# Differences of x made beside its sums, and a seventh weight unit for a raw tile and a sum tile

## The chip, the cores and the metric

The kernel runs on one core of one Trainium2 chip. The metric is the device time of one execution in microseconds. The kernel before took 1086.38 us (median of three runs, 1085.44 to 1087.5). A core has five engines with instruction streams of their own: TensorE (PE, with its weight loads PEld), VectorE (DVE), ScalarE (ACT), GpSimd (POOL) and SyncE (SP, which here only issues DMAs). Each works through its stream in the order in which the program was compiled, and they wait for each other by semaphores.

## The reference

One step of a two-layer encoder on 512 + 64 = 576 tokens of width 1024. Layer 0 mixes tokens by causal pooling, layer 1 by attention over selected keys; each is followed by an MLP. Cut to what matters here:

```python
def _mlp(h, w_up, w_down):          # h: (B, T, 1024), w_up: (1024, 4096), w_down: (4096, 1024)
    u = jax.nn.relu(h @ w_up)
    return (u * u) @ w_down
...
for i in range(DEPTH):              # DEPTH = 2
    h = _rmsnorm(x, norm_mix[i])
    ...                             # pooling mixer or attention
    x = x + y.astype(x.dtype)
    x = x + _mlp(_rmsnorm(x, norm_mlp[i]), mlp_w_up[i], mlp_w_down[i]).astype(x.dtype)
```

## The kernel before, in words

**Tiles.** Activations lie transposed: 128 of the 1024 features in the partitions, 576 tokens along the free axis, in two halves of HT = 288. `x[k]` is the residual's k-th block of 128 features (k from 0 to 7). Each fp32 operand of a matmul is split into a high part and the rest, both in the type float32r, and a product is three matmuls: high by high, high by low, low by high.

**Weights.** A weight block of 128 x 1024 is loaded as two raw tiles of 128 x 512 (`Stream.fill`, L199; the load is L213 on the SP queue for the MLPs). `split_unit` (L179) makes of each 128 x 512 piece a *unit*: ACT casts it to `wh` (L181), DVE subtracts to get `wl` (L182). A unit takes a pair of buffers out of a ring of UNITS = 6 pairs (`unit`, L169). Raw tiles come from two pools, RAWS = (4, 3): four `raws` for everything, three of `more` while an MLP or the pooling mixer runs. `fill` issues a load as soon as a raw tile is given back (`done`, L222).

**Sevens.** Most of an MLP is computed by a scheme with seven products in place of eight for a 2 x 2 block product (`seven`, L523). Its weight operands are made from a pair of blocks ("even" and "odd"), seven units for each pair in this order: a11, s1, s2, a12, s3, s2, a22 (`made`, L241). s3 comes about in the raw tile itself: POOL issues a DMA that adds the even block's first half onto the loaded raw tile (L217). s1 is loaded into a *sum tile* by SP (L237), and POOL's DMA adds the other half (L238). s2 is a sum tile too, made by DVE: s1 + a11 (L260), and, once it has been used for the first time, with a12 added (L264). The pool `sums` has four tiles.

The seven products of a seven go into three PSUM banks: a, b and c. The order is b11 into b (then ACT copies b to a, L533), t1 into c, t2 into b, b21 into a, t3 into b, b22 into c, t4 into b. After products a callback reads the bank. In the first matrix (`Up`, L586) `c` and `b` copy banks into `snap` (L599, L602, ACT); `lo0`, `hi1` (L612), `hi0` (L618) and `lo1` run relu and scale on DVE (L595), squares on ACT (L454), sums of the results on DVE (L484 to L491), and the splits of the results, upper on ACT (L473) and lower on DVE (L476). In the second matrix (`Down`, L555) every callback adds to or subtracts from the residual (L562, DVE). `take()` takes the next unit, `ahead()` (L509) makes one more unless `LEAD` units are ready.

**Chunks.** An MLP runs over four chunks of 1024 hidden features. Chunk 0's Up is eight plain blocks (`project`, L297, L677 to L691), followed by four Down sevens in the order FIRST_DOWN. Chunks 1, 2 and 3 are four Up sevens and four Down sevens each (in the last layer chunk 3 has three, and the rest goes with the final norm).

**Operands of x.** The sevens of Up need, for each of four pairs j (blocks j and j + 4 of x), three sums and one difference of scaled quarters of x. `x_sums` (L424) makes the three sums: ACT scales one quarter (L429, into `first`), DVE makes three scalar_tensor_tensors out of x (L430 to L432), and the result is split (L433, L434). This runs for j = 0 and 1 after plain blocks 3 and 5 (L689), in a tile `rough`, and for j = 2 and 3 after the first and second Down seven (`x_prepared`, L694). `x_difference` (L436) takes the split quarters out of `xs`: a subtraction of both parts at once (L439, 576 columns), the sum of the two results (L440), and the split (L441, L442) over the quarter in `xs` that is no longer needed. All four j run after the third Down seven. `snap` is the buffer of the norm's sum of squares (tag "s2"), allocated after the plain blocks (L692).

**Order.** Only some parts of the kernel have an order written by hand. In the MLPs the framework puts each engine's instructions in order by its own simulated timeline, with the program's order as priority, so that an instruction whose operands are ready can be put ahead of earlier ones. A tile is allocated when an earlier tile of its pool has been given back.

**Memory.** Pools lie on top of each other like a stack. `more` lies at the bottom during layer 0's MLP; in attention `under` takes its place, with the cosine table `cs`, the sine table `sn`, a mask and one score tile (6144 bytes per partition, like three raw tiles).

## Time and profile before

| | us |
|---|---|
| median of three runs | 1086.38 |
| lowest, highest | 1085.44, 1087.5 |
| the profiled execution | 1085.9 |
| its span, first to last instruction | 1084.1 |
| PE busy in the span | 1051.9 |
| DVE busy | 909.1 |
| ACT busy | 627.1 |
| POOL busy | 264.6 |

The page names the engine, the line and the tiles of instructions: `wl<-raw,wh` is an instruction that writes `wl` from `raw` and `wh`. "Busy" is the time in which an engine executes; an arrow in square brackets gives idle time of the engine just before an instruction, and what ended it. PE's matmuls overlap, so that a record of 0.30 us follows the one before it after 0.13 us.

In time the span divides so: pooling mixer until about 41 us; layer 0's plain Up blocks until 95, its chunks until 414; attention until about 690; layer 1's MLP with the final norm until the end. The DMA queues moved 157.66 MB, a mean of 145 GB/s.

### The profile page before, as it was taken

The numbers are of one execution on the slowest core, as the hardware profiler recorded it, in microseconds if no ns is written. First come the engines' busy times: TensorE is split into PE (matmuls) and PEld (weight loads), VectorE is DVE, ScalarE is ACT, GpSimd is POOL, SyncE is SP. The second block draws the span as 40 slices with busy tenths as digits, with TensorE's granted clock in tenths as the row PEclk, the third lists the DMA queues.
The fourth block names the chain that finished last, engine by engine and source line by source line (L and its number), as shares of the span: only waits on it lengthen the run. The fifth ranks groups of instructions, "written<-read, shape, count | busy, mean of one in ns | idle before, by whom it ended". The sixth has DMA issues, their size and how long they took to land.

```text
span 1084.1 us, 21647 instructions
## 1 busy us (share of the span) xinstructions
PE 1051.9 (97%) x7942; PEld 1024.0 (94%) x7942; DVE 909.1 (84%) x1845; ACT 627.1 (58%) x1240; POOL 264.6 (24%) x285
## 2 busy tenths in 40 slices
PE   9999999999999999999999999999999999999996
PEld 8999998999999999999988888999999999999895
DVE  7788989879978987869999944688989879979974
ACT  8555466447546654444477776455467447547641
POOL 4100111111111100237686892000111111111001
PEclk9999999999999999999989999999999999999998
DMA  8343676676676654447632454333676666667512
GB/s 252 94 102 89 171 166 151 166 163 169 151 166 165 156 161 165 128 153 191 201 108 68 129 170 123 126 108 97 166 165 157 162 164 165 154 170 161 125 51 88
DMA packets 94459, 157.66 MB, mean 145 GB/s; under 512 B 13729, under 2 KB 25296, under 8 KB 94352
## 3 DMA queue, kind: packets, MB, share of 16 engines
q1 hardware_dynamic: 68720, 109.80, 33.3%
q0 software_dynamic: 15840, 28.84, 17.1%
q10 hardware_dynamic: 9792, 17.63, 5.2%
q8 instruction: 62, 1.02, 0.4%
q14 instruction: 45, 0.37, 0.1%
HBM read 141.15 MB, written 10.89 MB: 140 GB/s over the span
## 4 chain that ended last, share of the span: by engine, by line
PE 78%; DVE 9%; ACT 3%; POOL 3%; issue 3%; DMA 2%; SPq 0%; DVEq 0%; POOLq 0%; ACTq 0%
PE b L504 28%; PE c L504 15%; PE up L305 9%; PE a L504 7%; PE pj L305 7%; PE wo L305 2%; DVE wl L182 2%; PE wa L305 1%; PE pb L1011 1%; PE sc L1284 1%; PE dn L305 1%; PE pt L1310 1%; POOL p L1263 1%; DVE u L476 1%; PE o L1342 1%
## 5 line engine op out<-in xcount | busy, mean ns | idle before, releaser
L181 ACT CAST wh<-raw 128x512 fp32r<-128x512 f32 (+1 forms) x316 | 194.8, 620 | 232.6 <-PE b L504 75.4
L182 DVE TENSOR_TENSOR wl<-raw,wh 128x512 fp32r<-128x512 f32 (+1 forms) x294 | 205.9, 703 | 38.6 <-ACT wh L181 30.2
L504 PE MATMUL b<-u,wh 128*128 128x288 f32 x992 | 203.1, 296 | 2.2 <-ACT a L533 1.7
L504 PEld LDWEIGHTS b<-u,wh 128*128 128x128 f32 x992 | 159.5, 188 | 4.3 <-ACT a L533 3.6
L181 ACT CAST wh<-sum 128x512 fp32r<-128x512 f32 x165 | 101.4, 620 | 80.3 <-PE b L504 36.3
L504 PE MATMUL b<-u,wl 128*128 128x288 f32 x496 | 145.5, 296 | 0.0
L182 DVE TENSOR_TENSOR wl<-sum,wh 128x512 fp32r<-128x512 f32 x165 | 112.0, 687 | 20.6 <-ACT wh L181 18.5
L238 POOL DMA_DIRECT2D sum<-in_w_down x31 | 27.1, 891 | 327.4 <-DVE u L476 86.6
L504 PE MATMUL c<-u,wh 128*128 128x288 f32 x496 | 103.3, 297 | 0.9 <-DVE u L476 0.6
L504 PEld LDWEIGHTS b<-u,wl 128*128 128x128 f32 x496 | 92.8, 188 | 0.0
L305 PE MATMUL up<-xs,wh 128*128 128x288 f32 x512 | 89.6, 296 | 1.0 <-DVE x L1477 0.8
L504 PE MATMUL b<-xt,wh 128*128 128x288 f32 x384 | 77.9, 296 | 8.0 <-DVE v L612 8.0
L476 DVE TENSOR_TENSOR u<-v,u 128x864 fp32r<-128x864 f32 (+2 forms) x100 | 82.1, 825 | 0.9 <-ACT u L473 0.5
L504 PEld LDWEIGHTS c<-u,wh 128*128 128x128 f32 x496 | 80.1, 188 | 2.5 <-DVE x L562 1.5
L473 ACT CAST u<-v 128x864 fp32r<-128x864 f32 (+2 forms) x100 | 72.7, 730 | 8.8 <-DVE v L491 5.4
L504 PE MATMUL b<-xs,wh 128*128 128x288 f32 x384 | 76.8, 295 | 0.0
L305 PEld LDWEIGHTS up<-xs,wh 128*128 128x128 f32 x512 | 74.6, 188 | 2.0 <-ACT wh L181 1.0
L504 PE MATMUL c<-u,wl 128*128 128x288 f32 x248 | 73.2, 295 | 0.0
L238 POOL DMA_DIRECT2D sum<-in_w_up x24 | 20.7, 863 | 209.4 <-DVE wl L182 132.5
L504 PEld LDWEIGHTS b<-xt,wh 128*128 128x128 f32 x384 | 61.3, 188 | 9.6 <-DVE v L612 9.6
L454 ACT ACTIVATE v<-v 128x288 f32<-128x288 f32 (+1 forms) x112 | 52.0, 476 | 16.5 <-DVE v L595 14.1
L305 PE MATMUL pj<-xs,wh 128*128 128x288 f32 x352 | 61.3, 295 | 0.0
(287 smaller groups left out, 2738.4 us busy)
## 6 DMA issues: line engine op xcount, KB each, us to landing
raw<-in_w_up SPq DMA_DIRECT2D x128, 256.0 KB, 3.0
raw<-in_w_down SPq DMA_DIRECT2D x128, 256.0 KB, 2.9
raw<-in_w_o ACTq DMA_DIRECT2D x32, 256.0 KB, 2.8
sum<-in_w_down SPq DMA_DIRECT2D x31, 256.0 KB, 2.9
sum<-in_w_down POOLq DMA_DIRECT2D x31, 256.0 KB, 4.5
raw<-in_w_down POOLq DMA_DIRECT2D x31, 256.0 KB, 5.0
raw<-in_w_in ACTq DMA_DIRECT2D x30, 256.0 KB, 3.0
sum<-in_w_up SPq DMA_DIRECT2D x24, 256.0 KB, 3.0
```

The costliest lines, as they stand in the source:

```text
L181: act.copy(h, src)
L182: how["sub"].tensor_tensor(l, src, f32(h), ALU.subtract)
L238: pool.dma_start(s1, odd[:, 512:], accum_op=ALU.add)
L305: pe.matmul(pt[h][:, :m] if isinstance(pt, tuple) else pt[:, h, :m], wt, xs[k][:, part, c:c + m], start=(k == 0 and i == 0), stop=(k == n ...
L454: act.activation(v, v, AF.Square)
L473: act.copy(u[:, f, 0], v[:, f])
L476: dve.tensor_tensor(u[:, f, 1], v[:, f], f32(u[:, f, 0]), ALU.subtract)
L504: pe.matmul(bank[:, :HT], wt, ut, start=first and j == 0 and i == 0, stop=j == 3 and i == 2, skip_group_check=True)
L1011: pe.matmul(pt[:, c0:c0 + rhs.shape[1]], lhs, rhs, start=n == 0, stop=n == len(steps) - 1)
L1263: pool.tensor_scalar(p, p, rs[:, h:h + 1], 1.0, ALU.mult, ALU.mult)
L1284: pe.matmul(pt[:, hh, :nw], q[:, 2 * s + hh], ks[g][:, part, :nw], start=part == 0, stop=part == 1)
L1310: pe.transpose(pp[:, c:c + P], pr[:, hh, kt * P:(kt + 1) * P], ident)
```

## The change

Four things change together.

1. `x_sums` gets one more output, the difference: a scalar_tensor_tensor out of x and `first` (gain of block j + 4 times its first quarter, minus `first`). `x_difference` only splits what was made there. For j = 0 and 1 the difference waits in `snap`, which is therefore allocated after plain block 3; for j = 2 and 3 it lies in the fifth row of the scratch tile. `x_difference` now runs for j = 0 and 2 after the first Down seven and for j = 1 and 3 after the second, and no longer after the third.
2. A pool `extra` with one pair of weight buffers exists during the MLPs, and every seventh MLP unit is put there, so that the ring has seven pairs. LEAD goes from 5 to 6.
3. The pool `more` has two raw tiles and not three, `sums` three and not four. One raw tile and one sum tile have the size of the pair of weight buffers.
4. `under` must have the size of two raw tiles: the sine table moves into the pool `cst2`, and a pad of 64 columns that nobody uses fills up.

```diff
--- before.py
+++ after.py
@@ -44,10 +44,11 @@
 UNITS = 6
 SPREAD_AT = 5
 SPARE_UNITS = 6
-RAWS = (4, 3)
+UNDER = 64
+RAWS = (4, 2)
 MLP_BLOCKS = ("up", "even", "odd", "down")
 SEEDED = 4
-LEAD = 5
+LEAD = 6
 UP_ORDER = (0, 4, 1, 5, 2, 6, 3, 7)
 FACTORS = ("t4", "t3", "t1", "t2", "b11", "b22", "b21")
 FIRST_DOWN = (0, 2, 1, 3)
@@ -134,7 +135,7 @@
         def __getitem__(self, k):
             return self.t[k // 2][:, k % 2]
 
-    turns = {"spare": 0}
+    turns = {"spare": 0, "extra": 0}
 
     def raw_tile(pool=raws, n=2 * 264):
         return pool.tile([P, n], F32, tag="raw", name=uid("raw"))
@@ -166,8 +167,12 @@
     ready = []
     how = {"sub": dve}
 
-    def unit(n=512):
-
+    def unit(n=512, mlp=False):
+
+        if mlp and "extra" in phase:
+            turns["extra"] += 1
+            if turns["extra"] % (UNITS + 1) == 0:
+                return [phase["extra"].tile([P, n], F32R, tag=t, name=uid(t)) for t in ("wh", "wl")]
         return [weights.tile([P, 528], F32R, tag=t, name=uid(t))[:, :n] for t in ("wh", "wl")]
 
     def spare_unit():
@@ -176,8 +181,8 @@
         t = slot("cd"[turns["spare"] % 2], "w")
         return [t[:, i * 512:(i + 1) * 512] for i in range(2)]
 
-    def split_unit(src, spare=False):
-        h, l = spare_unit() if spare else unit(src.shape[1])
+    def split_unit(src, spare=False, mlp=False):
+        h, l = spare_unit() if spare else unit(src.shape[1], mlp)
         act.copy(h, src)
         how["sub"].tensor_tensor(l, src, f32(h), ALU.subtract)
         return h, l
@@ -250,7 +255,7 @@
             kind, raw = block[:2]
             if kind != "even":
                 for i in range(2):
-                    u = split_unit(raw[i], kind == "w_kq" and i == 0 and turns["spare"] < SPARE_UNITS)
+                    u = split_unit(raw[i], kind == "w_kq" and i == 0 and turns["spare"] < SPARE_UNITS, kind in MLP_BLOCKS)
                     stream.done(raw[i])
                     yield u
                 continue
@@ -259,7 +264,7 @@
             s2 = phase["sums"].tile([P, 512], F32, tag="sum", name=uid("sum"))
             dve.tensor_tensor(s2, s1, a11, ALU.add)
             for n, src in enumerate((a11, s1, s2, a12, s3, s2, a22)):
-                u = split_unit(src)
+                u = split_unit(src, mlp=True)
                 if n == 3:
                     dve.tensor_tensor(s2, s2, a12, ALU.add)
                 if n in (0, 3, 4, 6):
@@ -421,25 +426,22 @@
 
             return (KT - LAST if end and c == 3 else KT) // 2
 
-        def x_sums(j, raw, first):
+        def x_sums(j, raw, first, difference):
 
             t = x_sums_tile()
             xt.append(t)
             gain, minus = gv[:, gi, j:j + 1], negative[:, half + j:half + j + 1]
             act.activation(first, x[j][:, :HT], AF.Copy, scale=gain)
             dve.scalar_tensor_tensor(raw[:, 0], x[j][:, HT:], gain, first, ALU.mult, ALU.subtract)
+            dve.scalar_tensor_tensor(difference, x[half + j][:, :HT], gv[:, gi, half + j:half + j + 1], first, ALU.mult, ALU.subtract)
             dve.scalar_tensor_tensor(raw[:, 1], x[half + j][:, :HT], minus, raw[:, 0], ALU.mult, ALU.subtract)
             dve.scalar_tensor_tensor(raw[:, 2], x[half + j][:, HT:], minus, raw[:, 1], ALU.mult, ALU.subtract)
             act.copy(t[:, :, 0], raw)
             dve.tensor_tensor(t[:, :, 1], raw, f32(t[:, :, 0]), ALU.subtract)
 
-        def x_difference(j, snap):
-
-            b12, b22 = xs[j][:, :, :HT], xs[half + j][:, :, :HT]
-            dve.tensor_tensor(snap, f32(b22), f32(b12), ALU.subtract)
-            dve.tensor_tensor(snap[:, 0], snap[:, 0], snap[:, 1], ALU.add)
-            act.copy(b12[:, 0], snap[:, 0])
-            dve.tensor_tensor(b12[:, 1], snap[:, 0], f32(b12[:, 0]), ALU.subtract)
+        def x_difference(j, difference):
+
+            split(xs[j][:, :, :HT], difference)
 
         def of_x(j, factor, part):
             if factor[0] == "b" or factor == "t3":
@@ -688,20 +690,17 @@
             todo.clear()
             if i in (3, 5):
                 r = 2 * i - 6
-                x_sums(i // 2 - 1, rough[:, r:r + 3], rough[:, r + 3])
-        snap = halves(tmp("snap", "s2", 1))
+                if i == 3:
+                    snap = halves(tmp("snap", "s2", 1))
+                x_sums(i // 2 - 1, rough[:, r:r + 3], rough[:, r + 3], snap[:, i // 2 - 1])
 
         def x_prepared(n):
 
             if n < 2:
                 v = v_tile()
-                x_sums(n + 2, v[:, :3], v[:, 3])
-            elif n == 2:
-                for j in range(half):
-                    if j % 2 == 0:
-                        v = v_tile()
-                    i = j % 2 * 2
-                    x_difference(j, v[:, i:i + 2])
+                x_difference(n, snap[:, n])
+                x_sums(n + 2, v[:, :3], v[:, 3], v[:, 4])
+                x_difference(n + 2, v[:, 4])
 
         for n, q in enumerate(FIRST_DOWN):
             seven(of(us), n == 0, Down(q))
@@ -1059,7 +1058,8 @@
         for j in range(KT // 2):
             nc.sync.dma_start(xd[:, 2 * j:2 * j + 2], x.t[j])
         cst = phase["cst2"]
-        cs, sn = (const([P, T], s, pool=phase["under"]) for s in ("cs", "sn"))
+        cs, sn = const([P, T], "cs", pool=phase["under"]), const([P, T], "sn", pool=cst)
+        const([P, UNDER], "pad", pool=phase["under"])
         nc.sync.dma_start(cs, a["cos"])
         nc.sync.dma_start(sn, a["sin"])
         V = const([P, 9, 256], "V", pool=cst)
@@ -1480,12 +1480,12 @@
     with stage(more=RAWS[1]):
         with stage(xs=1, slots=1, tmps=6, ps=3, po=2):
             pool_mixer()
-        with stage(xs=1, u=1, acts=1, xt=1, sums=4, ps=2, po=4):
+        with stage(xs=1, u=1, acts=1, xt=1, sums=3, extra=1, ps=2, po=4):
             mlp(0, 1, late=KT)
     with stage(under=1, xs=1, queries=1, slots=1, cst2=1, tmps=5), ExitStack() as parts:
         parts.enter_context(stage(ps=2, po=4))
         attention(parts)
-    with stage(u=1, xs=1, acts=1, xt=1, sums=4, more=RAWS[1], ps=2, po=4):
+    with stage(u=1, xs=1, acts=1, xt=1, sums=3, extra=1, more=RAWS[1], ps=2, po=4):
         mlp(1, 3, end=last)
```

## The prediction

> **What bounds the kernel now.** I read the page's totals first, then the busy time by stage, then what the matmul engine waits for, and last the order of VectorE's work around the longest of these waits.
>
> ```profile
> span 1084.1 us, 21647 instructions
> PE 1051.9 (97%) x7942; PEld 1024.0 (94%) x7942; DVE 909.1 (84%) x1845; ACT 627.1 (58%) x1240; POOL 264.6 (24%) x285
> ```
>
> TensorE (PE) is busy for 97% of the span, so at most 32 us can be won without removing matmuls, and the change removes none. VectorE (DVE) is next. What matters is where PE's few idle microseconds lie. The next view gives busy time in stretches that I chose: six of 55 us, one for each chunk's four Up sevens and the hand-over to Down (chunks 1, 2, 3 of layer 0, then of layer 1), and three of the Down sevens ahead of them. Columns: busy us of PE, weight load, DVE, ACT, POOL, then clock, DMA share, GB/s.
>
> ```profile
> 140.00:195.00 55.00, 52.40 (x388) 51.26 (x387) 50.17 (x97) 36.98 (x74) 7.80 (x9) 1.00 0.65 157
> 231.50:286.50 55.00, 53.73 (x401) 52.87 (x400) 50.79 (x98) 37.68 (x76) 7.86 (x10) 1.00 0.64 154
> 322.70:377.70 55.00, 53.72 (x401) 52.84 (x400) 50.80 (x98) 37.67 (x76) 7.79 (x9) 1.00 0.63 156
> 788.10:843.10 55.00, 52.70 (x392) 51.70 (x391) 50.22 (x97) 36.71 (x74) 7.77 (x9) 1.00 0.65 160
> 879.50:934.50 55.00, 53.70 (x401) 52.80 (x400) 50.84 (x98) 37.52 (x75) 7.57 (x9) 1.00 0.63 157
> 971.20:1026.20 55.00, 52.74 (x393) 51.72 (x392) 50.94 (x99) 38.65 (x81) 6.94 (x8) 1.00 0.63 149
> 97.00:140.00 43.00, 42.83 (x324) 42.59 (x323) 42.18 (x83) 22.92 (x44) 6.91 (x8) 1.00 0.65 156
> 195.00:231.50 36.50, 36.50 (x277) 36.50 (x276) 29.43 (x54) 15.16 (x27) 6.04 (x7) 1.00 0.75 173
> 747.00:788.10 41.10, 41.10 (x310) 41.10 (x311) 40.37 (x79) 21.69 (x40) 6.94 (x8) 1.00 0.64 155
> ```
>
> In the Down stretches PE loses nothing or 0.17 us. In the six Up stretches it is idle for 2.60, 1.27, 1.28, 2.30, 1.30 and 2.26 us, 11.0 together. That is all the MLPs have to give, and chunk 1 loses more than chunk 2: 1.33 us more in layer 0 and 1.00 in layer 1. It is also chunk 1 that follows a stretch in which DVE was busy for 98% (42.18 of 43.00, 40.37 of 41.10) and not 81% (29.43 of 36.50). These two rows are where x's sums and differences are made.
>
> ```profile
> PE b L504 <- DVE v L612: 8.0, 7, 1.3
> PE b L504 <- ACT a L533: 1.7, 5, 1.0
> ```
> ```profile
> ACT wh L181 <- PE b L504: 111.8, 125, 2.7
> ```
>
> Waiter, what it waits for, us in total, times, longest. PE's idle time in the MLPs is one wait above all: a product into bank b until `Up.hi1` has read that bank (L612). No row has PE in an Up stretch waiting for a split weight (`wh`, `wl`). It is the other way round: ScalarE's casts of weights (L181) wait for PE to give a buffer back. Now DVE at the last Up of chunk 2, and PE there (start, length, instruction):
>
> ```profile
> 275.33 0.69 DVE L260 TENSOR_TENSOR sum<-sum,raw 128x512 f32<-128x512 f32 x1
> 275.93 0.69 DVE L182 TENSOR_TENSOR wl<-raw,wh 128x512 fp32r<-128x512 f32 x1
> 276.53 0.68 DVE L264 TENSOR_TENSOR sum<-sum,raw 128x512 f32<-128x512 f32 x1
> 277.13 0.45 DVE L595 SCALAR_TENSOR_TENSOR v<-a,rbm 128x288 f32<-128x288 f32 x1
> 277.50 0.45 DVE L618 TENSOR_TENSOR v<-c,snap 128x288 f32<-128x288 f32 x1
> 277.87 0.45 DVE L612 TENSOR_TENSOR v<-b,snap 128x288 f32<-128x288 f32 x1
> ...
> 281.41 0.68 DVE L182 TENSOR_TENSOR wl<-sum,wh 128x512 fp32r<-128x512 f32 x1
> ```
> ```profile
> 272.56 0.30 PE L504 MATMUL a<-xs,wl 128*128 128x288 f32 x1
> ...
> 278.37 0.53 PE L504 MATMUL b<-xt,wh 128*128 128x288 f32 x2 [1.11 <-DVE v L612]
> ```
>
> Bank a was full at 272.9; DVE read it (L595) at 277.13, 4.3 us late. In between stand weight splits and sums for products that are still far off, back to back at 0.60 us. So PE loses its time to DVE's order and load, not to a missing weight.
>
> **The change part by part.** *Differences of x.* Per layer and pair j, L439 and L440 go and one scalar_tensor_tensor comes, of the form of L430; the split behind (L441, L442) stays.
>
> ```profile
> L439 DVE TENSOR_TENSOR v<-xs,xs x8: 748/751/752, 119.6 to 778.1; 128x576 f32<-128x576 f32 x8
> ```
> ```profile
> L440 DVE TENSOR_TENSOR v<-v x8: 448/450/453, 122.9 to 781.7; 128x288 f32<-128x288 f32 x8
> ```
> ```profile
> L430 DVE SCALAR_TENSOR_TENSOR v<-x,gv,v x4: 509/514/516, 102.2 to 759.1; 128x288 f32<-128x288 f32 x4
> ```
>
> 4 x (0.751 + 0.450 - 0.514) is 2.75 us of records per layer; records overlap the next by about 0.09 (0.69 long, 0.60 apart), which leaves 2.4 us per layer. Two of the four additions go to the plain Up blocks ahead of 97 us, where PE runs on its own matmuls with DVE behind it; so the stretch 97 to 140 is freed of some 3.3 us and falls from 98% to about 90% of DVE. PE does not wait there, so the direct gain is nothing. The gain, if any, is that DVE comes to chunk 1's Up with weights split further ahead, as it does to chunks 2 and 3: bounded by chunk 1's excess, 1.33 + 1.00 = **2.3 us**, and by nothing below. I take all of it in the forecast. The splits of the differences now come one to two sevens earlier. What they overwrite was last read by the plain Up blocks, so they wait for no matmul. For j = 0 and 1 the difference lies in `snap`, which takes the norm's buffer; its writer would wait on DVE for the norm's sums on PE, done after block 1, while it is issued after block 3: nothing is queued behind it. Cost nothing.
>
> *LEAD 6.* The last plain block leaves 4 units ready; each seven takes 7 and calls `ahead` 7 times, so `ready` goes back to 4 and `len(ready) < 5` is always true. Raising it changes nothing. What acts is the ring of buffers: 7 and not 6 lets a cast start one product earlier. No PE wait ends on a weight, so the direct gain is nothing. Indirectly it cuts both ways: one split more can be done ahead of the Up sevens (0.60 us less DVE in them), or one more can be put in front of L612 (0.60 us later). At six hand-overs that is -3.6 to +3.6 us.
>
> *One sum tile less.* A sum tile is taken by L237's load (s1) or by L260 (s2).
>
> ```profile
> L260 DVE TENSOR_TENSOR sum<-sum,raw x55: 682/689/695, 57.9 to 1023.7; 128x512 f32<-128x512 f32 x55
> ```
>
> ```profile
> 267.79 0.33 SPq L237 DMA_DIRECT2D sum<-in_w_down  x1
> ...
> 282.12 0.33 SPq L237 DMA_DIRECT2D sum<-in_w_down  x1
> ```
>
> The L260 at 275.33 is for the next seven, made while the old s2 is unfinished (its second split is the L182 of 281.41), the next s1 is held and the one behind it is being loaded (267.79): four tiles, and the next load goes out as that split ends (282.12). With three, this L260 must run after 281.41, or the load of 267.79 comes later. It leaves the place in front of L612, a gain of 0.60 us at each hand-over; it may then stand before the last L476, which Down waits for, a loss of 0.69. Ring and sums together lie between -3.6 and +4.1 us; I take -0.6, one split's distance for all six hand-overs together, since the two effects oppose each other.
>
> *One raw tile less.* For one seven's third raw block: the slot given back by a split on DVE, the load on SP, the accumulation on POOL, and the cast.
>
> ```profile
> 304.20 0.69 DVE L182 TENSOR_TENSOR wl<-raw,wh 128x512 fp32r<-128x512 f32 x1
> ```
> ```profile
> 304.92 8.28 SPq L213 DMA_DIRECT2D raw<-in_w_up  x4
> ```
> ```profile
> 308.36 0.86 POOL L217 DMA_DIRECT2D raw<-in_w_up  x1 [0.70 <-DVE wl L182]
> ```
> ```profile
> 322.64 0.62 ACT L181 CAST wh<-raw 128x512 fp32r<-128x512 f32 x1 [0.96 <-PE b L504]
> ```
> ```profile
> raw<-in_w_up POOLq DMA_DIRECT2D x24, 256.0 KB, 4.8
> ```
>
> Landed at 308.36 + 4.8 = 313.2, used at 322.6: 9.4 us to spare. Four raw blocks a seven of 11.1 us make one slot 2.8 us on average (here the next split ends at 306.5, 1.6 later). Some 6 us stay. SP and POOL issue in order, so the sums' loads queued behind move by as much, and they have more to spare. Cost nothing; without that cover a cast, and PE behind it, would lose up to 2.8 us a seven.
>
> *sin in another pool, and the pad.* One load on SP comes earlier or later by its region's release; the first use is two projections into attention. Nothing, at most one transfer's 3 us.
>
> **The sum:** -2.3 - 0.6 = -2.9 us. The profiled execution took 1085.9 us (span 1084.1 and 1.8 around it), 0.5 less than the median of 1086.4. So 1083.0 on its scale, **1083.5** on the median's.
>
> **The rivals.** *Freed time that nobody waits for.* Against my 2.3 us stands this:
>
> ```profile
> 142.16 0.69 DVE L182 TENSOR_TENSOR wl<-raw,wh 128x512 fp32r<-128x512 f32 x1 [0.94 <-ACT wh L181]
> 144.64 0.46 DVE L562 TENSOR_TENSOR x<-x,b 128x288 f32<-128x288 f32 x1 [1.79 <-PE b L504]
> ```
>
> DVE had 2.7 us to itself just before chunk 1's first `relu`, so it had caught up and carried nothing over; the 1.3 us of the later waits then belongs to the order inside the Up sevens. The time stays at 1086.4.
>
> *The sum tile bites (slower).* L260, held until s2's second split, falls between L612 and the last L476 at the Up-to-Down hand-over, in front of the parts that Down's products need. Price 0.69 us at six hand-overs, 4.1 us: 1090.5. It decides if L260 starts before the last L476 there; if it starts after, it is free, since DVE is idle for 7.1 of the 36.5 us of Down from 195.
>
> *The bubble is a missing weight buffer.* Were the repeated wait on bank b really for the ring, the seventh unit would take away its 8.0 us: 1078.4. The rows speak against it: the releaser is L612, and the wait is for a PSUM bank, of which the change adds none. [...]
>
> **How the numbers follow.** Forecast 0.43, missing buffer 0.03, nobody waits 0.31, the sum tile bites 0.23. A measurement here tells 0.2%, 2.2 us, from no change: faster 0.46, same 0.31, slower 0.23. The forecast's own range is 1080.5 (2.3 + 3.6 gained) to 1084.2. The range over the cases is 1080.0 to 1091.0; it leaves out the missing buffer and mishaps in attention, where a new order of instructions is possible as well.
>
> **What would show it.** DVE's busy time about 5 us lower; L439 and L440 gone. In the forecast, the stretches of chunk 1 lose about 1.3 us like those of chunk 2, and no L260 stands between the last two L612 of a chunk's hand-over. If the idle rows of all six stretches are unchanged, the first rival is right; if L533, L476 or L473 appear as releasers of PE at the hand-overs, the second. The prediction is wrong altogether if PE waits for `wh`, `wl` or a load, or if the change lies outside the MLPs.

## The result, and the profile after

The changed kernel takes 1097.51 us (median of four runs, 1095.04 to 1099.9). The kernel before, on the same chip, takes 1086.68 (four runs). The ratio is 1.0098, with a 95% interval of 1.0082 to 1.0114: about 11 us slower, where the prediction had 3 us faster and a range that ended at 1091. The profiled execution took 1099.35 us, span 1097.6.

The page of the changed kernel, its totals (busy us, share of the span, number of instructions for each engine):

```profile
span 1097.6 us, 21649 instructions
PE 1053.7 (96%) x7942; PEld 1024.0 (93%) x7942; DVE 904.7 (82%) x1837; ACT 628.8 (57%) x1240; POOL 263.7 (24%) x285
```

DVE's busy time fell by 4.4 us and its instructions by 8, as the new differences have it (2 x 4 in place of 4 x 4). PE does the same 7942 matmuls. No engine has more instructions in its row than before, and the span is 13.5 us longer: it went into waits, and into stretches in which PE ran slower (below). PE's waits in the changed kernel (waiter, what it waits for, us in total, times, longest; L614 is `hi1`, L478 `lower`, L464 `activated`):

```profile
PE b L506 <- DVE v L614: 9.9, 6, 2.0
PE b L506 <- DVE u L478: 3.0, 4, 0.8
PE c L506 <- DVE x L564: 2.4, 5, 0.5
...
PE up L310 <- DVE v L464: 1.1, 1, 1.1
...
PE b L506 <- ACT wh L186: 0.4, 2, 0.2
```

The wait for `hi1`'s read of bank b was 8.0 us and is 9.9. Two releasers that were small before have grown: the lower parts (L478) at the hand-over to Down, and updates of the residual (L564) in the Down sevens behind it. In the MLPs PE waits for a `wh` for 0.4 us, and for no `wl` and no load. Here is the third Up seven of chunk 2, first DVE (start, length, instruction):

```profile
264.49 0.68 DVE L187 TENSOR_TENSOR wl<-sum,wh 128x512 fp32r<-128x512 f32 x1
...
265.83 0.68 DVE L187 TENSOR_TENSOR wl<-sum,wh 128x512 fp32r<-128x512 f32 x1
...
266.80 0.68 DVE L187 TENSOR_TENSOR wl<-raw,wh 128x512 fp32r<-128x512 f32 x1
267.40 0.68 DVE L269 TENSOR_TENSOR sum<-sum,raw 128x512 f32<-128x512 f32 x1
268.00 1.05 DVE L478 TENSOR_TENSOR u<-v,u 128x864 fp32r<-128x864 f32 x1
268.97 0.68 DVE L187 TENSOR_TENSOR wl<-raw,wh 128x512 fp32r<-128x512 f32 x1
269.57 0.75 DVE L478 TENSOR_TENSOR u<-v,u 128x576 fp32r<-128x576 f32 x1
270.24 0.68 DVE L187 TENSOR_TENSOR wl<-sum,wh 128x512 fp32r<-128x512 f32 x1
270.98 0.69 DVE L187 TENSOR_TENSOR wl<-raw,wh 128x512 fp32r<-128x512 f32 x1
271.59 0.45 DVE L597 SCALAR_TENSOR_TENSOR v<-a,rbm 128x288 f32<-128x288 f32 x1
271.95 0.45 DVE L614 TENSOR_TENSOR v<-b,snap 128x288 f32<-128x288 f32 x1
```

and PE there:

```profile
265.38 0.29 PE L506 MATMUL a<-xs,wl 128*128 128x288 f32 x1
...
270.13 0.29 PE L506 MATMUL b<-xs,wl 128*128 128x288 f32 x1
272.46 0.53 PE L506 MATMUL b<-xt,wh 128*128 128x288 f32 x2 [2.04 <-DVE v L614]
```

Bank a is full at 265.7 and read at 271.59, 5.9 us late (4.3 in the last Up seven of this chunk before). Between the two, DVE starts five weight splits and a sum for later products, beside its work on the results of the seven before. PE's t4 product waits 2.04 us; the longest such wait before was 1.3. PE stands still as long from 175.9 and from 364.9, in the third Up seven of chunks 1 and 3. All three are in layer 0.

After two of those three stalls something follows that the profile of before shows in attention (granted clock 0.50 from 561.88 to 572.12 us) and at its end (0.50 from 1077.3), but nowhere in the sevens. Busy time by stretches (length; busy us of PE, weight load, DVE, ACT, POOL; granted clock, DMA share, GB/s):

```profile
178.00:182.00 4.00, 4.00 (x19) 4.00 (x20) 2.56 (x6) 2.01 (x6) 0.00 (x0) 0.57 0.66 178
182.00:186.00 4.00, 4.00 (x33) 4.00 (x32) 3.60 (x8) 3.19 (x7) 0.65 (x1) 1.00 0.34 95
...
273.90:277.30 3.40, 3.40 (x17) 3.40 (x16) 2.84 (x7) 2.18 (x5) 0.00 (x0) 0.51 0.19 45
277.30:282.00 4.70, 4.70 (x37) 4.70 (x37) 3.31 (x6) 3.74 (x7) 0.86 (x1) 1.00 0.53 122
...
367.00:371.00 4.00, 4.00 (x30) 4.00 (x31) 3.46 (x8) 2.29 (x6) 0.00 (x0) 1.00 0.36 124
```

PE is busy throughout, but at half the clock, with 19 matmuls in 4 us and not 33. By estimate each such stretch costs 1.5 to 1.7 us: at its exact borders it has 16 matmuls in 3.41 us (178.22 to 181.63, 273.79 to 277.20), where 33 in 4 us make 28, and half of 3.41 is 1.7.

### The profile page after: what moved, and what is told of

The parts are those of the page before. It is cut to its first block, busy times and chain, and to the rows that moved or that the text cites. A ratio compares the mean times of both kernels' runs of the same rounds, so it can differ in the third digit from the quotient of the medians.

```text
span 1097.6 us, 21649 instructions
## 1 busy us (share of the span) xinstructions
PE 1053.7 (96%) x7942; PEld 1024.0 (93%) x7942; DVE 904.7 (82%) x1837; ACT 628.8 (57%) x1240; POOL 263.7 (24%) x285
## 4 chain that ended last, share of the span: by engine, by line
PE 76%; DVE 11%; DMA 4%; issue 4%; POOL 2%; ACT 2%; SPq 0%; DVEq 0%; POOLq 0%; ACTq 0%
PE b L506 28%; PE c L506 14%; PE up L310 9%; PE a L506 7%; PE pj L310 4%; PE wo L310 3%; DVE wl L187 3%; PE wa L310 2%; PE sc L1284 1%; PE pb L1010 1%; PE pt L1310 1%; PE v L1184 1%; DVE u L478 1%; PE dn L310 1%; DMA sum<-in_w_down 1%
## 5 line engine op out<-in xcount | busy, mean ns | idle before, releaser
L222 POOL DMA_DIRECT2D raw<-in_w_down x31 | 26.7, 863 | 364.7 <-DVE u L478 81.4
L478 DVE TENSOR_TENSOR u<-v,u 128x864 fp32r<-128x864 f32 (+2 forms) x100 | 81.6, 825 | 6.6 <-ACT u L475 6.4
L222 POOL DMA_DIRECT2D raw<-in_w_up x24 | 20.7, 863 | 205.7 <-DVE wl L187 103.3
L564 DVE TENSOR_TENSOR x<-x,b 128x288 f32<-128x288 f32 x93 | 41.7, 450 | 27.1 <-PE b L506 27.0
```

Source lines behind the costliest of these rows:

```text
L222: pool.dma_start(raw[0], self.even[:, :512], accum_op=ALU.add)
L478: dve.tensor_tensor(u[:, f, 1], v[:, f], f32(u[:, f, 0]), ALU.subtract)
L564: dve.tensor_tensor(to, to, self.banks[bank], op)
```

## The experiments

All 7942 matmuls are in every profile, so the time between two of the same number can be compared between kernels (PE's order of products differs a little, which blurs the borders by tenths). The table gives that for the profiled execution of each, in us against the kernel before: the plain Up blocks of both layers (matmuls 280 to 681 and 5128 to 5529), the first Down sevens of both (681 to 1010, 5529 to 5860), the chunks behind them (1010 to 3010, 5860 to 7760), and everything else (mixer, attention, w_o, the end). "New" are the new differences; units, raw tiles, sum tiles follow; "H" is the sum held behind the last lower part, "P" the first sum held in the plain stage (both below). Time and ratio with its interval are those of the repeated runs.

| run | kernel | us | ratio | plain Up | first Down | chunks | rest |
|---|---|---|---|---|---|---|---|
| after | new, 7, 4+2, 3 | 1097.51 | 1.0098 [1.0082, 1.0114] | +1.0 | +2.2 | +9.1 | +1.2 |
| e1 | new, 6, 4+3, 4 | 1086.31 | 0.9996 [0.9987, 1.0004] | 0.0 | +2.2 | -2.6 | +1.0 |
| e2 | old, 7, 4+2, 3 | 1092.53 | 1.0052 [1.0037, 1.0067] | +0.9 | +2.2 | +3.8 | -2.2 |
| e3 | new, 6, 4+2, 3 | 1095.59 | 1.0075 [1.0059, 1.0092] | +4.1 | +2.2 | +2.8 | +1.1 |
| e4 | new, 7, 4+1, 4 | 1109.68 | 1.0212 [1.0195, 1.023] | +1.3 | +3.1 | +17.0 | +2.7 |
| e5 | new, 6, 4+2, 4 | 1094.4 | 1.0068 [1.0051, 1.0085] | +2.3 | +2.2 | -2.6 | +6.1 |
| e6 | new, 6, 4+3, 3 | 1090.29 | 1.0034 [1.0023, 1.0045] | 0.0 | +2.1 | +1.8 | +0.9 |
| e10 | e6 with H | 1085.38 | 0.9996 [0.9985, 1.0007] | -0.1 | +2.2 | -0.7 | -1.2 |
| e11 | e5 with P | 1087.69 | 1.0018 [1.0002, 1.0035] | 0.0 | +1.2 | -3.0 | +1.9 |
| e12 | after with H, P | 1091.4 | 1.0045 [1.0028, 1.0062] | 0.0 | +1.9 | +5.7 | -3.7 |
| e13 | e12, splits held | 1099.02 | 1.0108 [1.0095, 1.0122] | -0.1 | +1.9 | +12.1 | -0.4 |
| e14 | e3 with H, P | 1086.84 | 1.0003 [0.9989, 1.0017] | -0.1 | +2.5 | -0.8 | -0.8 |
| e15 | e1 with H, P | 1081.21 | 0.9952 [0.994, 0.9965] | 0.0 | +1.0 | -4.0 | -0.9 |
| e16 | e15, splits held | 1111.99 | 1.0234 [1.022, 1.0248] | 0.0 | +1.1 | +25.0 | +0.4 |
| e17 | before with H, P | 1082.28 | 0.9966 [0.9954, 0.9978] | 0.0 | +0.1 | -2.9 | -0.9 |
| e18 | e1 with H | 1085.05 | 0.9997 [0.9987, 1.0007] | +0.1 | +2.2 | -4.5 | +1.5 |

The rest moves between -3.7 and +2.7 (e5 apart), and not by edits alone: e12 differs from after by almost 5 there, with no edit in it. Attention's instructions come out in another order in every kernel, and PE's clock adds to it: in attention it runs at half clock for 10.2 us in the profile of before, and over the whole span the granted clock is 0.992 there and 0.997 in e10's. What either is worth was not tried by itself. One profile stands for each kernel, so a row of the table need not add up to the difference of the medians.

### The parts alone: e1 to e4

e1 takes all but the differences out of the change, e2 takes the differences out, e3 the seventh unit, and e4 gives the fourth sum tile back for another raw tile:

```diff
 # e1: RAWS = (4, 3), LEAD = 5, sums=4, no extra, sin where it was
 # e2: x_sums, x_difference and x_prepared as before
 # e3
-        if mlp and "extra" in phase:
+        if False and mlp and "extra" in phase:
 # e4
-RAWS = (4, 2)
+RAWS = (4, 1)
-        with stage(xs=1, u=1, acts=1, xt=1, sums=3, extra=1, ps=2, po=4):
+        with stage(xs=1, u=1, acts=1, xt=1, sums=4, extra=1, ps=2, po=4):
```

> The differences of x made along with the sums, and nothing else of the change: six weight units, 4 + 3 raw tiles, four sum tiles. DVE's order in chunk 1's Up sevens then becomes that of chunks 2 and 3. Theory A (the seventh unit, by DVE's order, makes the loss): PE's idle time in chunk 1 falls to chunk 2's 1.3 us in both layers, about 2.3 us faster than before, 1084, and DVE about 5 us less busy. Theory B (fewer raw and sum tiles make the loss): the same 1084 here. Theory C (the new place of the differences, earlier and in the busy plain blocks, makes the loss): most of the 10.8 us here, 1094 to 1098.

> The seventh unit, paid with a raw tile and a sum tile, with the differences made in the old way. Theory A: slow, 1094 to 1100; PE waits 2 us or more for L612's counterpart in the third Up seven. Theory B: as slow as that too. Theory C: about as before, 1085 to 1089.

> The whole change, but no unit is ever put into the extra pair of buffers: the ring has six units, while raw tiles (4 + 2), sum tiles (3) and differences are those of the change. Theory A: near the differences alone, 1083 to 1088. Theory B: as slow as the change, 1095 to 1100. It tells A from B.

> The whole change with the memory paid otherwise: a ring of seven, four sum tiles as before, and 4 + 1 raw tiles. Theory A: slow like the change, 1093 to 1100, since the ring has seven units. Theory B by the sum tile: about 1084 to 1087; B by the raw tile: slower than the change, over 1100.

The differences alone change nothing in the median (e1), where two of the theories had 1084. Without the seventh unit the change still costs 9.3 us over e1 (e3), so my first theory, that the unit does it, fell as the main cause; in the median the unit adds 1.9. In the chunks, though, it adds 6.2 (9.1 against 2.8). The parts don't add up. Where the unit is in, the wait in layer 1's plain stage that e3 has is gone. And e2 fits no theory: with the old differences the change costs 5.0 us less, though the new ones alone cost nothing. Of the 5.2 that e2's chunks are shorter, up to 3.4 can be the slow clock, by estimate: the chunks of after have two stretches of it, and over the span the granted clock is 0.993 in e2's profile against 0.992. Where e2's slow clock lies was not shown. In e4, DVE waits at the sum (L265) for loads of `w_up` for 22.2 us and of `w_down` for 16.4: with one raw tile more taken, loads are really late. Of the differences, e1 shows both halves of the account. PE's waits in e1:

```profile
PE b L505 <- DVE v L613: 6.5, 6, 1.1
PE b L505 <- ACT a L534: 3.1, 6, 1.0
```

Chunk 1 loses its excess, as forecast (8.0 us of waits for `hi1` become 6.5; the time from matmul 1010 on falls by 2.6 in the two layers). But the copy of b to a (L534), which ACT makes at the start of a seven, was waited for by 1.7 us and is now by 3.1. In the first Down sevens ACT now also has the casts of the moved splits:

```profile
104.19 0.43 ACT L295 CAST xs<-v 128x288 fp32r<-128x288 f32 x1
104.53 0.61 ACT L185 CAST wh<-raw 128x512 fp32r<-128x512 f32 x1
105.52 0.38 ACT L534 COPY a<-b 128x288 f32<-128x288 f32 x1 [0.38 <-PE a L533]
```

and PE's next product into b follows at 105.96, after an idle 0.47. In both layers the first Down sevens are 1.1 us longer. That the cast alone does it was not shown: ACT is idle for 0.38 ahead of the copy, so PE's own order plays a part, and e2, with the old differences, has the 2.2 too.

### Raw tile or sum tile: e5 and e6

```diff
 # e5: e1 with
-RAWS = (4, 3)
+RAWS = (4, 2)
 # e6: e1 with
-        with stage(xs=1, u=1, acts=1, xt=1, sums=4, ps=2, po=4):
+        with stage(xs=1, u=1, acts=1, xt=1, sums=3, ps=2, po=4):
```

> Alone against the kernel with the new differences (1086.3): one raw block tile less in each MLP (4+2), ring of six units, four sum tiles. Theory A (the raw tile makes the loss: a load starts a slot later, and the sums of the plain Up blocks and of the sevens wait for it on DVE): most of the 9.3 us that raw and sum tile cost together, 1092 to 1096, with more waits of L265 and of the casts for raw loads. Theory B (the sum tile makes the loss): 1086 to 1087.5, PE waits for the same releasers as before, since DVE's order in the Up sevens is that of the kernel with the new differences.

> Alone against the kernel with the new differences (1086.3): three sum tiles, raw tiles 4+3, ring of six. Theory B (the sum tile makes the loss, by the order of DVE's sums and splits that the scheduler chooses for it: splits and sums of the next seven stand between bank a filled and its read): 1093 to 1096, PE waiting for L613 (hi1) by more than 8 us a run and for L477 (lower) at the hand-over to Down. Theory A (the raw tile): 1086 to 1088.

Both cost, e5 8.1 us and the sum tile 4.0. They cost in different places. One raw tile less takes nothing in the chunks (-2.6 in e5 as in e1), where the prediction had looked. It takes 2.3 in the two plain Up stages and 5.1 in the rest, 3.5 of it where the MLP ends and attention's projections begin (matmuls 3010 to 3100).

Those 3.5 us are not the raw tile's price in the change. e5 leaves the sine table in `under`, so that `under` is larger than `more`; so it is in e4, and in e11 below. These three lose 3.3 to 3.5 us there, and every other kernel of the table 0.1 at most, after included. In these three attention's first product runs behind the last one of Down; in the others it runs some 40 matmuls or more ahead of it. So moving the sine table, as the change does, avoids this loss. That the larger pool makes attention's first tiles wait for tiles of the MLP is likely, but was not tried. What a raw tile costs with the table moved is read from e6 to e3: 5.3 us. The plain stage of layer 0 in e1, DVE:

```profile
58.28 0.69 DVE L264 TENSOR_TENSOR sum<-sum,raw 128x512 f32<-128x512 f32 x1 [0.62 <-DMA raw<-in_w_down]
...
62.17 1.42 DVE L463 SCALAR_TENSOR_TENSOR v<-up,rbm 128x576 f32<-128x576 f32 x2 [2.26 <-ACT rbm L340]
```

and in e5:

```profile
63.33 0.69 DVE L264 TENSOR_TENSOR sum<-sum,raw 128x512 f32<-128x512 f32 x1 [2.74 <-DMA raw<-in_w_down]
63.94 1.41 DVE L463 SCALAR_TENSOR_TENSOR v<-up,rbm 128x576 f32<-128x576 f32 x2
```

The block of `w_down` that this sum reads gets its raw tile later. Its load goes out, on SP's queue, in e1 at

```profile
55.39 0.33 SPq L217 DMA_DIRECT2D raw<-in_w_down  x1
```

and in e5 at

```profile
60.61 0.33 SPq L217 DMA_DIRECT2D raw<-in_w_down  x1
```

That is 5.2 us later, of which 0.7 is the lag of the whole kernel there. PE doesn't need the sum until the first Down seven at 95 us. But it stands on DVE ahead of the reads of the plain blocks' banks (L463). These could have run at about 62.9, by estimate: in e1 they start at 62.17, when ACT's copy of `rbm` is done, and e5 lags by 0.7. PE waits for a bank:

```profile
64.74 0.80 PE L309 MATMUL up<-xs,wh 128*128 128x288 f32 x4 [1.17 <-DVE v L463]
```

For the sum tile, the second rival has the price exactly: 1090.29 against its 1090.5. Its place is there too. At the hand-over of chunk 2 in e6, DVE has

```profile
284.46 0.69 DVE L264 TENSOR_TENSOR sum<-sum,raw 128x512 f32<-128x512 f32 x1
285.06 1.72 DVE L477 TENSOR_TENSOR u<-v,u 128x864 fp32r<-128x864 f32 x2
```

the sum right in front of the last lower part. Whether that is the cause is what e10 asks.

### One order for DVE: e7, e8 and e9

The three kernels (before, after, e1) with DVE's instructions of the sevens in the program's order:

```diff
+        with tc.manual_schedule(engines={ENG.DVE}):
             for n, q in enumerate(FIRST_DOWN):
                 seven(of(us), n == 0, Down(q))
                 x_prepared(n)
...
```

> The kernel before with DVE's instructions of the Down and Up sevens kept in the order of the program (the sums and splits of a unit right behind the product that asked for them, the bank reads where the program has them), nothing else changed. It has no outcome of its own to tell; it is the yardstick for the next one: this order and the buffers of before. Theory of order: 1083 to 1092, since each bank read stands at its product. Theory of buffers: about 1086, DVE's order not being what matters.

> The changed kernel with DVE's instructions of the sevens in the order of the program, the same sequence as in the yardstick. Buffers are then the only difference in the sevens (seven units, 4+2 raw, 3 sums, and the new differences). Theory of order (the loss comes from the order of DVE's work that was chosen for the new buffers, not from any buffer being late): within 2 us of the yardstick or below it. Theory of buffers (loads and sums are really late with one tile less): 8 to 11 us above the yardstick, with the waits of L269 and L187 for loads to show for it.

> The new differences alone (six units, 4+3 raw, 4 sums) with DVE's instructions of the sevens in the order of the program. Between the kernel before (1155.5) and the changed kernel (1144.9) in that same order it parts the 10.6 us into the differences and the buffers. Theory of order: the buffers cost nothing once the order is fixed, so this run lies at or above 1144.9. Theory of buffers: one raw and one sum tile less cost some 9 us in any order, so this run lies about 1136.

1155.49 us (ratio 1.0629 [1.0613, 1.0644]), 1144.86 (1.0532 [1.0516, 1.0549]) and 1139.39 (1.0492 [1.0463, 1.052]). Neither theory holds whole. In one and the same order the new buffers cost 5.5 us, about half of the 11.2 that they cost in the framework's order (1097.51 against e1's 1086.31). The differences gain 16.1 there. And the order itself is worth 47 to 69 us in each kernel, more than any buffer, where 1092 at most was expected of e7: the framework's order is by far the better one. The clock blurs these three: over the span of their profiles the granted clock was 0.977 (e7), 0.985 (e8) and 0.981 (e9), against 0.992 in that of before. If all of it is half clock, that is 53, 34 and 43 us of it, by estimate, against 17.

### One instruction held back: e10, e11 and e12

H and P add an ordering edge between two instructions of DVE, and no wait:

```diff
+    def behind(inst, key):
+        first = held.pop(key, None)
+        if first is not None:
+            tc.add_manual_dep(inst.ins, first.ins.name, ..., reason=key)
...
-            dve.tensor_tensor(s2, s1, a11, ALU.add)
+            total = dve.tensor_tensor(s2, s1, a11, ALU.add)
+            behind(total, "lower")
+            behind(total, "activated")
...
                 if self.final:
+                    held["lower"] = last_part
                     ahead(2)
```

`last_part` is the last lower part of a chunk's last Up seven; "activated" is the read of the third plain block's banks.

> The kernel with three sum tiles (1090.3), with one edit: at each hand-over from Up to Down the sum s2 of the next seven (L264 there) may not be issued on DVE ahead of the last lower part (L477 there). Theory (the second rival of the prediction: the sum in front of the last lower part is what three sum tiles cost, 0.69 us at six hand-overs): 1086 to 1087.5. If the loss is the whole shifted order inside the Up sevens, of which this sum is one piece: 1088 to 1089, the first Down product's wait at each hand-over some 0.35 us shorter and the wait for hi1's read unchanged. If the sum's place is not the cause: 1090.

> The kernel with one raw tile less (1094.4), with one edit: in each plain Up stage the first sum of Down's weights may not be issued on DVE ahead of the third block's bank reads. Theory (the load of that sum's raw block goes out a slot later, and on DVE the bank reads stand behind the sum that waits for it): the wait of PE for L463 (activated) goes in both layers, 1.1 and 1.2 us, 1092. If the weights behind the sum are then late themselves: 1094 or more, PE waiting at the first Down seven.

> The changed kernel with both edits (the sum behind the last lower part at the hand-overs, the first sum of Down's weights behind the third plain block's bank reads). If these two places are most of its loss: 1092 or less. If most of it is the weight splits that the seventh unit lets stand in front of bank reads, with the PE stall of 2.3 us in the third Up seven: 1094 to 1096.

In the plain stages P does what was expected: the 2.3 us are gone in e11. The kernel fell to 1087.69, further than the 1092 that was expected, because the first Down sevens fell by 1.0 and the rest by 4.2, where nothing was edited. The 3.5 us at attention's entry stay. So the sum's place in DVE's order, in front of reads that were ready, turned a late load into PE's wait.

H brings e6 from 1090.29 to 1085.38, a little below what the theory had, but the table forbids the easy reading. With four sum tiles H gains as well (e1 to e18: 1.9 in the chunks; e6 to e10: 2.5), and 2.1 of the 4.9 us came in the rest, where nothing was edited. With H in both, three tiles still cost 3.8 in the chunks (e10 against e18), where they cost 4.4 without it. So the sum in front of the last lower part is 0.6 of the 4.4. The wait view of 240 to 300 us (chunk 2) says where most of it lies, in e10

```profile
PE b L513 <- DVE v L621: 1.6, 2, 1.3
```

and in e18

```profile
PE b L513 <- DVE v L621: 0.6, 1, 0.6
```

1.0 more in this chunk, waiting for `hi1`, and 5.0 in the whole run (8.3 against 3.3): the shifted order inside the Up sevens. There the rival's price was met by another mechanism than its own.

With both holds the changed kernel (e12) takes 1091.4, as the first branch had it. Of the 9.5 us between its profile and that of after, 4.8 lie in the rest, and some 1.7 of the 3.4 in the chunks may be one stretch less at half clock: e12 has one at 177.6 to 181.0 us (0.50), and over the span its granted clock is 0.994 against 0.992. By this estimate about 3 us are left for the holds themselves.

### What the seventh unit costs: e13 and e14

e13 holds, in Up sevens, each weight split that the program has behind a read of bank a or b:

```diff
-        how["sub"].tensor_tensor(l, src, f32(h), ALU.subtract)
+        rest = how["sub"].tensor_tensor(l, src, f32(h), ALU.subtract)
+        if how["sub"] is dve:
+            behind(rest, "read")
...
-                self.relu(4, self.banks[0], ALU.max, 1)
+                held["read"] = self.relu(4, self.banks[0], ALU.max, 1)
                 ahead()
```

e14 is e3 with H and P.

> The changed kernel with the two edits of before (sums held, 1091.4) and a third: in an Up seven, a weight split that the program has behind a read of bank a (lo0) or of bank b (hi1) may not be issued on DVE ahead of that read. Theory (what the seventh unit costs is the splits that it lets stand in front of bank reads): the PE stall of 2.33 us at the third Up seven falls under 1.4, and the time to 1084 to 1087. If holding the splits back makes the weights late instead: PE waits for wl, 1092 or more.

> The whole change but for the seventh unit (ring of six, 1095.6 as it was), with the sum held at the hand-overs and the first sum of Down's weights held in the plain Up stages. If the raw and the sum tile cost no more than those two places: 1085 to 1088, and what the kernel with both edits and the seventh unit still loses (1091.4) is the seventh unit's alone. If raw and sum tile together cost something that neither does alone: 1090 or more.

With H and P, all that is left of the change without its seventh unit is 1086.84, level with the kernel before (though 5.6 above e15, which has the full buffers). The seventh unit on top of that is 4.6 us in the median and 6.5 in the chunks, as it was 6.2 there without the holds. That it costs is shown. How is shown by half only. With the splits held, the stall ahead of t4 in layer 0 (2.04 us of waiting, 2.33 from the start of one matmul to the next) is gone and layer 0's chunks fall from 5.0 above before to 1.5. In layer 1 they rise from 0.7 to 10.5, where half clock comes in (0.50 from 849.5 to 852.5 us), and where PE now waits, from 740 us on, for

```profile
PE b L517 <- DVE wl L187: 4.2, 6, 1.2
```

The splits in front of the reads cause the stall, and there is not enough time behind the reads to make them: DVE's order has to thread both, and a fixed rule does it worse than the framework did.

### A version that beats both: e15 to e18

e15 is e1 with H and P, e16 that with the splits held, e17 the kernel before with H and P, e18 is e1 with H alone.

> The new differences alone, buffers of before (1086.3), with the same two holds. In the kernel with one raw tile less the hold also took about 0.5 us off each layer's first Down sevens, where the new differences give back what they win in chunk 1. If that is the hold's doing here too: 1084.5 to 1086, a little under the kernel before. If it was that kernel's order alone: 1086.3.

> The same as the last, and in the Up sevens no weight split ahead of the bank read that the program has in front of it. Theory of order: the stall of 1.35 to 1.41 us before the last t4 product, the largest that is left in each chunk, gets shorter: 1079 to 1084. If the splits are needed where they stood, PE waits for wl: 1087 or more.

> The kernel before (old differences, buffers of before) with both holds. If the 5 us that the kernel with the new differences and both holds is under the kernel before are the holds' alone: 1081 to 1083. If the new differences are a part of it (they give back in the first Down sevens, about 1 us a layer, what they win in chunk 1, unless the hold is there): 1083 to 1085.

> The new differences with the hold at the hand-overs alone, without the hold in the plain Up stages (1081.2 with both, 1086.3 with none). If the shorter stall before the last t4 product comes from the hold at the hand-overs: 1082 to 1083, and the first Down sevens stay 1.1 us a layer above those of before. If the plain stage's hold makes the gain: 1085 to 1086.

e15 beats both kernels: 1081.21 us, ratio 0.9952 [0.994, 0.9965], faster than either branch had. It needs nothing of the new buffers. PE's longest wait in the MLPs is now

```profile
PE b L514 <- DVE v L622: 3.3, 6, 0.6
```

where it was 8.0, 7, 1.3. Two edges that hold one sum each do most of it: e17, without the new differences, takes 1082.28, ratio 0.9966 [0.9954, 0.9978]. The two intervals overlap. The differences gain 1.1 in the chunks (-4.0 against -2.9) and give 1.0 back in the first Down sevens; whether they are worth anything stays open. H alone (e18) takes 1.9 off the chunks, but the median only from 1086.31 to 1085.05: its rest is 0.5 longer than e1's, and e15's 1.9 shorter. By its time e18 met the branch of the plain stage's hold, but its wait for `hi1` is 3.3 us as in e15, so the shorter stall comes from H. e16 failed as e13 did: PE waits 17.1 us for `wl`.

## Why the prediction was wrong

**What bounds the kernel** was read rightly: PE's few idle microseconds come from DVE's order, with bank reads behind splits and sums, and not from a missing weight. The missing-buffer rival fell: with one weight buffer more the longest gap is 2.04 us and not 1.3. One more PSUM bank was not tried. What did not follow from the right reading is the next step. If the order makes the time, then an edit of buffers is an edit of the order, and every "costs nothing" that rests on the trace of before is without its ground.

**Differences.** The gain of 2.3 us in chunk 1 came (2.6 in the table for e1), and so did DVE's 4.4 us (about 5 were forecast). The sentence that failed is "Cost nothing" for the splits that come one to two sevens earlier: the first Down sevens grew by 2.2. That the splits do it is argued and not shown, since they grow as much in e2 without them. The first rival's 1086.4 was the time of this part alone, by another way than its own: the time was waited for, and was given back.

**LEAD, and the sine table.** LEAD is inert, as said: compiled with 5 and with 6, the instruction streams of the changed kernel are the same on all five engines. The sine table's new place cost nothing that is seen (after +0.1 us at attention's entry), and spared the 3.3 to 3.5 us of the kernels whose `under` is larger than `more`.

**One raw tile less.** The step said 9.4 us to spare and "Cost nothing". In the sevens that holds to 0.0 us. It failed by its scope: the same pool feeds the plain Up stages, where the slots carry the first blocks of Down ahead of time. There the load went out 5.2 us later in e5 (55.39 to 60.61), DVE reached the sum before its data, and the bank reads stood behind it. That is the very question that the prediction set itself for an added wait, who stands behind the waiting instruction, and did not ask in this stage. The term is 5.3 us (e6 to e3) where 0 stood, the largest of the three. 4.1 of it lie in the plain stages of e3's profile; 1.7 of these, by estimate, are a stretch at half clock behind the stall in layer 1 (0.51 from 718.6 to 722.0 us). In the profile of after, the plain stages lose 1.0 us only.

**One sum tile less and the ring.** -0.6 was chosen out of -3.6 to +4.1. The sum tile alone came out at +4.0, at the upper end, and the ring at +1.9 on top of raw and sum tile, or +4.6 where the holds are in. Together they are outside their own range, whose two parts had not been added because they were thought to oppose each other. The choice went by the row of before in which a sum stands in front of L612. That sum did leave the place in e6, and between 275.16 and 278.61 two lower parts, the other sum and two splits stand there. That the two effects oppose each other was wrong: both make the wait for `hi1`'s read longer, the sum tile from 6.5 to 8.2 us (e1 to e6), the ring from 8.2 to 9.9 (e3 to after).

On this path the three terms make up the loss: 4.0 for the sum tile (e1 to e6), 5.3 for the raw tile (e6 to e3) and 1.9 for the ring (e3 to after) are the 11.2 us between e1 and the changed kernel.

**The ranges.** The second rival, 1090.5, was the right side with the right price for its part. All rivals priced one part; none had two parts going wrong together.

## What to carry to other kernels

When a scheduler orders the engines' streams, a changed buffer count is a new program on every engine: price it in every stage that draws on the pool, and take "it had time to spare" for a statement on the old order alone. Before adding a buffer for a gap, look whether the releaser ran when its operands were ready; if it stood in its queue behind work for later, an ordering edge on that one instruction is the edit. Here two such edges were worth 4.2 us on the kernel before.

## What the runs showed of the hardware

Two of the three PE stalls of about 2 us in after are followed by 3.41 us at half clock (0.57 and 0.51 in the rows above, which are cut a little too wide for it). e3 has such a stretch from 718.6 to 722.0 us (0.51), and e12 from 177.6 to 181.0 (0.50). In the traces of before and after, the changes of the clock lie whole multiples of 3.413 us apart (a third of the 10.24 from 561.88 to 572.12 in before): in before 572.12 to 1077.29 is 148 of them; in after 181.63 to 273.79 is 27, 277.20 to 662.91 is 113 and 666.32 to 1089.58 is 124. Counted from the start of the span, the steps of after and those of before lie 1.4 us apart. Cut on the steps, the first and the third stall of after read:

```profile
174.80:178.22 3.42, 1.39 (x11) 1.15 (x10) 3.34 (x8) 1.67 (x4) 0.66 (x1) 1.00 0.87 168
178.22:181.63 3.41, 3.41 (x16) 3.41 (x16) 1.97 (x6) 1.42 (x4) 0.00 (x0) 0.50 0.72 198
...
362.55:365.96 3.41, 2.39 (x19) 2.16 (x17) 3.37 (x6) 1.82 (x4) 0.86 (x1) 1.00 0.85 177
365.96:369.37 3.41, 2.39 (x18) 2.39 (x19) 2.90 (x8) 1.82 (x5) 0.00 (x0) 1.00 0.74 212
```

The first stall has 2.04 us of waiting and falls into one step. It leaves PE busy for 1.39 us of it, and the next step runs at half clock. So it is with the second (1.37 us of the step from 270.38). The third, 2.03 us, falls across two steps, leaves 2.39 us in each, and nothing follows. Over the whole profile of after, the four steps ahead of half clock (174.80, 270.38, 659.50 and 1086.17) leave PE busy for 1.37 to 1.58 us of 3.41, and every other step at full clock from 4.14 us on for 2.04 us or more. In before the border is less sharp: the step from 558.47 has 2.13 us and half clock follows, the one from 172.76 has 2.09 and nothing does. And e13, where no wait of PE from 740 to 1060 us is longer than 1.2 us, has half clock there as well:

```profile
849.50:852.50 3.00, 3.00 (x14) 3.00 (x14) 3.00 (x6) 1.78 (x4) 0.18 (x1) 0.50 0.59 183
```

So in after, by the estimate above, two of the three stalls near 2 us cost 1.5 to 1.7 us more than themselves, and the two are those that fall into one step. In the changed kernel's profiled execution that is some 3 us of the 13.5. Whether its runs at 1095 and those at 1099 differ by these stretches was not shown, since only one of them has a profile; their granted clocks are 0.993 and 0.992 at 1095, 0.992 in both at 1099.
